# The normalised x of tokens 1024 to 2047 of a hybrid attention layer: turned by transposing DMAs instead of by TensorE

## The chip, the cores and the metric

One core of a Trainium2 chip. The metric is the device time of one execution in microseconds (us). TensorE (PE) multiplies and can transpose 128x128 blocks, VectorE (DVE), ScalarE (ACT) and GpSimd (POOL) work element by element, SyncE (SP) issues most DMAs. Every engine has its own queue and runs it in order.

## The reference

A decoder layer over 2048 tokens of width 1024, batch 1. Two attention mixers share one normalised, modulated input and one input projection:

```
xn = rms_norm(x, g_pre)                    # per token
h  = xn * (1 + scale(c)) + shift(c)        # per channel, the same for all tokens
q,k,v,f,z (mixer A), q,k,v,z (mixer B) = split(h @ w_in)
A: forgetting attention, 8 heads, causal, all 2048 keys
B: sliding window of 128 with sinks, 8 query heads, 2 key heads, rotary positions
out = x + gate(c) * rms_norm(concat(A * silu(z_A), B * silu(z_B)) @ w_out)
```

The change touches only how `h` comes to stand with channels on partitions, as the projections need it.

## The kernel before, in words

The tokens are cut into four chunks of 512 (`ci` 0 to 3), each into four tiles of 128 tokens x 1024 channels: `xt[0]` to `xt[15]`, loaded by `load_x` (L410). For each chunk `squares` (L417, ACT) sums x squared per token, `root` turns the sums into `rst` = 1/rms (a few small steps on DVE, then a chain on POOL, L108 to L122), and `normal` (L429, DVE) multiplies the tile by it.

`turn(ci, k)`, one of eight per chunk, brings channels k*128 to k*128+127 of the 512 tokens onto partitions: four PE transposes (L435) into `px`, ACT applies the channel's scale `Gp` and shift `Shp` into `hf`, float32 (L441; for even k also into the high part of `hT`), and DVE casts the high part for odd k (L445) and subtracts it from `hf` to give the low part (L446). `hT[ci]` holds both float16 parts, [128, 2, 8, 512]. A projection takes three products: high by high, low by high, high by low of the weight.

`hf` comes from a pool `hst` of three buffers with one tag. `px` comes from PSUM.

Then the projections of mixer B follow chunk by chunk: `kb(ci)`, keys, 24 matmuls (L351 with `wh_kb`); `vb(ci)`, values (L795); then one or more `zb` parts, the gate (L351 with `wh_zb`), whose weights are scaled and split shortly ahead (L267 on ACT, L273 on DVE). `kb(ci)` walks over k and at each k needs all 512 tokens of `hT[ci]`. After `kb` come rope steps: ACT copies the sums into `qf`, four DMAs turn halves around into `qs` (L751), DVE combines them with the tables `cosT` and `sinT` into `stb` (L754 to L765), and four DMAs store that to `kst` (L779). `spread(g)` (L460, L461) is eight loads of the tables of chunk g. Weights' maxima go through DRAM with stores of 4 bytes per partition, `mx_d` (L230), and come back as `mxr` (L235).

The order is written by hand. PE's work is a list of units, `punits`; the turns of the next chunk are set between units. Other work hangs on the number of a unit: `at_slice(n, f)` runs f there, and `after(n, f)` puts f some two units times n later, so that an engine's queue isn't given a step long before its input. The instructions then stand in each engine's queue in the order in which they were written. DMAs on SP signal completion on eight semaphores in turn, and a DMA is issued only when the one eight before it has landed.

Late in the kernel, transposing DMAs (L1483) already bring `o_d` from DRAM into `T`.

Of the kernel before, what the change touches and what calls it, by code (L numbers as in the profile page):

```python
# [43 lines left out]
def hybrid_layer(  # L44
# [32 lines left out]

    o_d = [dram.tile([CH, D], F32, name="o_d0")] + [dram.tile([4, 2, P, D], F16, name=f"o_d{t}") for t in range(1, NCH)]
    z_d = dram.tile([KT, P, S], F32, name="z_d")
    mx_d = [dram.tile([P, 1], F32, name=f"mx_d{n}") for n in range(3)]  # L80


# [58 lines left out]
    def early_pool(name, bufs):  # L141
        return early.enter_context(tc.tile_pool(name=name, bufs=bufs, side="right", reuse_waits="tile"))

    xin, hst, vbw = early_pool("xin", 4), early_pool("hst", 3), early_pool("vbw", 1)
    trig = early_pool("trig", 1)
    swx = ExitStack()
    swc = swx.enter_context(tc.tile_pool(name="swc", bufs=1))

# [53 lines left out]
    def after(n, f):  # L202
        late.append([n, f])
# [215 lines left out]
    def root(ci):  # L419
        ss, rst = rstd[ci]  # L420
        rsqrt_mean(rst, ss[:], 4, G if ci else None)

    def normal(ci, us=range(4)):
        for u in us:
            t, r = ci * 4 + u, rstd[ci][1][:, u:u + 1]
            if ci == 0:
                A.activation(xt[t], xt[t], AF.Copy, scale=r)
            else:
                V.tensor_scalar(xt[t], xt[t], r, None, op0=ALU.mult)  # L429
# [20 lines left out]
    def turn_x(ci, k):  # L450
        scaled, split = turn(ci, k)
        after(1, scaled)
        after(2, split)

    def spread(g):

        gr, gc = slice(32 * g, 32 * g + 32), slice(g * CH, (g + 1) * CH)
        for r in range(4):
            rr = slice(32 * r, 32 * r + 32)
            SP.dma_start(cosT[rr, gc], cs_[gr, :])  # L460
            SP.dma_start(sinT[rr, gc], (sp_ if r % 2 else sn_)[gr, :])  # L461
# [4 lines left out]
    with tc.manual_schedule():  # L466
# [207 lines left out]
            kaps[key] = kappa(pws[key], key)  # L674
        V.tensor_scalar(kf[:], kaps["vb"][:], PS_SCALE, None, op0=ALU.mult)
        normal(1, (0, 1))
        spread(0)
        for t in range(8, 12):
            load_x(t)
    start.close()  # L680
# [281 lines left out]
    def add(key, us):  # L962
        if key in ("va01", "va23"):
            for j in key[2:]:
                add(f"va{j}", [])
        elif key not in pkeys and key not in ("kb", "vb"):
            at = len(punits) - {"za3": 4}.get(key, 20 if key[:2] == "za" else 0)
            for n, (lead, f) in enumerate(((42, lambda: w_load(key, pieces(key))), (31, lambda: w_max(key)),
                                           (21, lambda: w_back(key)), (12, lambda: w_scale(key)),
                                           (9, lambda: w_high(key)), (7, lambda: w_low(key, 0)),  # L970
                                           (5, lambda: w_low(key, 1)), (4, lambda: w_done(key)))):
                if n >= 4 and key[:2] in ("qk", "za"):
                    lead -= 1
                if n < 4 and key == "qb0":
                    lead += (16, 14, 12, 4)[n]
                if key[:2] in ("zb", "va"):
                    lead += {"va0": 26, "va2": 26, "zb3": 18}.get(key, 8)
                if n == 0 and key in ("qk1", "za0"):
                    lead += 8
                if key == "zb1":  # L980
                    lead = at - (6, 38, 46, 67, 71, 73, 75, 77)[n]
                if key == "zb0":
                    if n >= 3:
                        events.setdefault((13, 13, 14, 15, 16)[n - 3], []).append(f)
                else:
                    events.setdefault(max(at - lead, n), []).append(f)
        if key not in pkeys:
            pkeys.append(key)
        punits.extend(us)
# [10 lines left out]
    def at_slice(n, f):  # L1000
        events.setdefault(n, []).append(f)
# [17 lines left out]
    for ci in range(NCH):  # L1019
        n0 = len(punits)  # L1020
        add("kb", kb_units(ci))
        add("vb", vb_units(ci))
        if ci < 3:
            add(*others[ci])
            if ci == 2:
                add(*others[4])
                add(*others[5])

            mine, punits[n0:] = punits[n0:], []
            at_ = ([14, 16, 17, 18, 19, 20, 21, 22], [6, 8, 10, 12, 14, 16, 18, 20], [14, 16, 18, 20, 22, 24, 26, 28])[ci]  # L1030
            for n, u in enumerate(mine):
                punits.append(u)
                if n in at_:
                    punits.append(lambda ci=ci, k=at_.index(n): turn_x(ci + 1, k))
            if ci < 2:

                for u in range(4):
                    at_slice(n0 + (24 if ci else 9) + u, lambda ci=ci, u=u: squares(ci + 2, (u,)))
                    at_slice(len(punits) + (4 if ci else -10) + u, lambda ci=ci, u=u: normal(ci + 2, (u,)))
                at_slice(len(punits) - (3 if ci else 18), lambda ci=ci: root(ci + 2))  # L1040
            at_slice((12, 22, 30)[ci], lambda ci=ci: spread(ci + 1))
    n0 = len(punits)
    at_slice(n0, lambda: open_fox())
# [740 lines left out]
```

## Time and profile before

| | us |
|---|---|
| median of 3 runs | 1157.98 (1157.04 to 1157.98) |
| profiled execution, its time | 1157.8 |
| its span | 1156.1 |
| PE busy, share of the span | 1116.8 (97%) |
| DVE busy | 930.5 (80%) |
| ACT busy | 661.4 (57%) |
| POOL busy | 207.5 (18%) |
| mean granted clock of PE | 0.996 of full |

Busy times are of instructions only; the time in which an engine waits is not in them. The part of the program that the change touches runs from about 20 to 130 us.

### The profile page before, as it was taken

What the parts mean: (1) busy time and instruction counts of PE and PEld (TensorE: products, weight loads), DVE (VectorE), ACT (ScalarE), POOL (GpSimd) and SP (SyncE); (2) the same over time, 40 slices, a digit from 0 to 9 for tenths busy, and PEclk for the clock granted to TensorE, in tenths of its full rate; (3) what the DMA queues carried; (4) which work ended last, traced back from release to release, by engine and by line L of the source; (5) the groups of instructions that cost most, each with busy time, mean ns of one, the idle gap of its engine ahead of it and who ended that gap; (6) DMA issues with size and microseconds to landing.
All of it is one profiled execution on the core that took longest, in us unless ns stands there. A gap on an engine that the chain in (4) does not pass through costs nothing. (4 is left out here: it accounts for less than half of the span.)

```text
span 1156.1 us, 25291 instructions
## 1 busy us (share of the span) xinstructions
PE 1116.8 (97%) x9869; PEld 656.3 (57%) x9869; DVE 930.5 (80%) x2137; ACT 661.4 (57%) x1150; POOL 207.5 (18%) x332
## 2 busy tenths in 40 slices
PE   5899999999999999999999999999999999999997
PEld 2475544577765866555555555555555555544444
DVE  7877468987888568788988899888888887878885
ACT  2876344654555421666757666666776778534332
POOL 1122134554556530010010110001000000000000
PEclk9899999999999999999999999999999999999999
DMA  9943355433243232442344342123311337686743
GB/s 333 336 116 72 87 78 96 97 63 90 52 92 88 58 87 58 73 108 29 80 64 87 84 67 70 38 49 76 45 43 34 91 101 206 140 225 197 199 135 109
DMA packets 123476, 120.10 MB, mean 104 GB/s; under 512 B 64948, under 2 KB 100828, under 8 KB 123356
## 3 DMA queue, kind: packets, MB, share of 16 engines
q1 hardware_dynamic: 112088, 85.69, 27.6%
q0 software_dynamic: 10832, 32.50, 13.5%
q8 instruction: 77, 1.26, 0.6%
q14 instruction: 43, 0.35, 0.1%
q10 hardware_dynamic: 436, 0.28, 0.1%
HBM read 64.75 MB, written 25.18 MB: 78 GB/s over the span
## 5 line engine op out<-in xcount | busy, mean ns | idle before, releaser
L1356 ACT ACTIVATE p<-sta,lift,scl_qk 128x1024 f32<-128x1024 f32 (+2 forms) x160 | 172.0, 1075 | 131.6 <-PE sta L1350 82.6
L351 PE MATMUL bk<-hT,wh_qk 128*128 128x512 f16 x768 | 194.7, 378 | 0.0
L1363 DVE TENSOR_TENSOR pha<-p,pha 128x1024 f16<-128x1024 f32 (+2 forms) x160 | 169.1, 1057 | 0.2 <-ACT pha L1360 0.2
L1303 DVE TENSOR_REDUCE a_m<-bk 128x1 f32<-128x512 f32 x192 | 130.4, 686 | 45.8 <-PE bk L1300 44.8
L1576 PE MATMUL bk<-wohl,oz 128*128 128x512 f16 x744 | 165.3, 379 | 1.1 <-DVE oz L1525 0.7
L1360 ACT ACTIVATE pha<-p 128x1024 f16<-128x1024 f32 (+2 forms) x160 | 148.1, 926 | 5.9 <-PE poa L1376 1.2
L1576 PEld LDWEIGHTS <-oz 128*128 128x128 f16 x744 | 71.9, 99 | 82.8 <-DVE oz L1525 1.8
L1376 PE MATMUL poa<-vt,pha 128*128 128x65 f16 x1088 | 116.1, 192 | 1.4 <-DVE pha L1363 1.2
L1373 PE MATMUL poa<-vt,pha 128*128 128x65 f16 x1088 | 116.6, 193 | 0.8 <-DVE ona L1382 0.7
L1375 PE MATMUL poa<-vt,pha 128*128 128x64 f16 x1088 | 116.6, 194 | 0.0
L351 PEld LDWEIGHTS <-wh_qk 128*128 128x128 f16 x768 | 72.1, 97 | 74.4 <-issue 2.1
L1349 PE MATMUL sta<-T 128*128 128x512 f16 (+1 forms) x320 | 110.9, 346 | 2.8 <-ACT p L1356 2.7
L1300 PE MATMUL bk<-T 66*128 66x512 f16 (+2 forms) x320 | 109.7, 348 | 2.4 <-DVE a_m L1303 1.9
L1373 PEld LDWEIGHTS <-pha 128*128 128x128 f16 x1088 | 101.5, 96 | 15.5 <-DVE ona L1382 1.9
L1350 PE MATMUL sta<-T 69*128 69x512 f16 (+1 forms) x320 | 109.8, 348 | 0.0
L1375 PEld LDWEIGHTS <-pha 128*128 128x128 f16 x1088 | 100.9, 97 | 11.4
L1376 PEld LDWEIGHTS <-pha 128*128 128x128 f16 x1088 | 100.8, 99 | 1.8 <-DVE pha L1363 1.7
L351 PE MATMUL bk<-hT,wh_za 128*128 128x512 f16 x384 | 99.7, 378 | 0.0
L369 PE MATMUL bk<-wh_va,hT 128*128 128x256 f16 x768 | 91.9, 273 | 0.0
L351 PE MATMUL bk<-hT,wh_zb 128*128 128x512 f16 x384 | 91.6, 379 | 0.2 <-DVE qc L754 0.2
L351 PE MATMUL bk<-hT,wh_qb 128*128 128x512 f16 x384 | 91.2, 379 | 0.0
L369 PEld LDWEIGHTS <-hT 128*128 128x128 f16 x768 | 73.3, 98 | 12.2 <-issue 2.1
(459 smaller groups left out, 1919.7 us busy)
## 6 DMA issues: line engine op xcount, KB each, us to landing
hT<-in_x_dram SPq DMA_DIRECT2D x20, 512.0 KB
wa<-in_w_ada_dram SPq DMA_DIRECT2D x16, 512.0 KB
z_d<-tz POOLq DMA_DIRECT2D x32, 256.0 KB, 3.0
T<-z_d SPq DMA_DIRECT2D x16, 512.0 KB
T<-stq SPq DMA_DIRECT2D x62, 128.0 KB
out_dram<-hT SPq DMA_DIRECT2D x15, 512.0 KB
xt<-in_x_dram SPq DMA_DIRECT2D x12, 512.0 KB
qs<-qf SPq DMA_DIRECT2D x80, 64.0 KB
```

Of the source, the lines that this page charges most:

```text
L351: PE.matmul(ps, whl[:, a, k, :], hT[ci][:, b, k, :], start=(k == 0 and n == 0), stop=(k == KT - 1 and n == 2))
L369: PE.matmul(ps[:, (u % 2) * 2 * P:(u % 2 + 1) * 2 * P], hT[ci][:, a, k, u * P:(u + 1) * P], wv[p][:, b, k, :], start=(k == 0 and n == 0), ...
L1303: V.tensor_reduce(m3[:, u, pc:pc + 1], mx[:, :w], axis=AX.X, op=ALU.max)
L1349: PE.matmul(self.st[:, o:o + w], T[:, 3, kb_], T[:, 1, qc], start=True, stop=False)
L1350: PE.matmul(self.st[:, o:o + w], T[0:XR, 2, kb_], T[0:XR, 0, qc], start=False, stop=not diag)
L1356: A.activation(self.p32[:, :self.w], self.st[:, :self.w], AF.Exp, scale=scl[f"qk{self.hd}"][:], bias=lift[:])
L1360: A.activation(self.ph[:, 0, :self.w], self.p32[:, :self.w], AF.Copy)
L1363: V.tensor_tensor(self.ph[:, 1, :self.w], self.p32[:, :self.w], self.ph[:, 0, :self.w], op=ALU.subtract)
L1373: PE.matmul(po[:, u, :], ph[:, 0, pq], vt[:, b, hd, 0:65], start=(self.first and n == 0 and u == 0), stop=False)
L1375: PE.matmul(po[:, u, 0:64], ph[:, 0, pq], vt[:, b, hd, 65:VW], start=False, stop=False)
L1376: PE.matmul(po[:, u, :], ph[:, 1, pq], vt[:, b, hd, 0:65], start=False, stop=(self.last and n == len(self.blocks) - 1))
L1576: PE.matmul(py, self.hl[:, i, k, :], w_slot(8 * j + k)[:, cc], start=(k == 0 and m_ == 0), stop=(k == KT - 1 and m_ == 2))
```

## The change

For chunks 2 and 3 (tiles `xt[8]` to `xt[15]`) the turns, and `normal`, are gone. `flat(ci, u)` takes their place, one per tile of 128 tokens, while tokens are still on partitions: DVE multiplies by `rst` and by `rowG`, the scales as one row repeated over partitions; the shifts `rowS` are added (POOL for chunk 2, DVE for chunk 3); ACT copies the result to a float16 tile `hh`, the high part; DVE subtracts it into a second `hh`, the low part; and SP issues two transposing DMAs from the two `hh` into `hT[ci]`. Below, T(ci,u) are these two DMAs, and low(ci,u) and hi(ci,u) the two steps that feed them.

`rowG` and `rowS` come about by a round trip: SP stores `Gp` and `Shp` to DRAM (`g_d`), 128 partitions x 8 pieces of 4 bytes each, ahead of `spread(0)`, and loads them back with a partition broadcast after it. `hh` shares tag and pool, so the three buffers, with `hf`. `squares`, `root` and the four steps of `zb1`'s weights get other slots. Line numbers shift; the function names above hold for both.

```diff
@@ -77,6 +77,7 @@
 
     o_d = [dram.tile([CH, D], F32, name="o_d0")] + [dram.tile([4, 2, P, D], F16, name=f"o_d{t}") for t in range(1, NCH)]
     z_d = dram.tile([KT, P, S], F32, name="z_d")
+    g_d = dram.tile([2, D], F32, name="g_d")
     mx_d = [dram.tile([P, 1], F32, name=f"mx_d{n}") for n in range(3)]
 
 
@@ -142,7 +143,8 @@
         return early.enter_context(tc.tile_pool(name=name, bufs=bufs, side="right", reuse_waits="tile"))
 
     xin, hst, vbw = early_pool("xin", 4), early_pool("hst", 3), early_pool("vbw", 1)
-    trig = early_pool("trig", 1)
+    trig, rowp = early_pool("trig", 1), early_pool("rowp", 1)
+    rowG = rowp.tile([P, D], F32, name="rowG")
     swx = ExitStack()
     swc = swx.enter_context(tc.tile_pool(name="swc", bufs=1))
 
@@ -451,6 +453,21 @@
         scaled, split = turn(ci, k)
         after(1, scaled)
         after(2, split)
+
+    def flat(ci, u):
+
+        t, r = ci * 4 + u, rstd[ci][1][:, u:u + 1]
+        parts = [hst.tile([P, D], F16, tag="hf", name="hh") for _ in range(2)]
+        V.scalar_tensor_tensor(xt[t], xt[t], r, rowG[:], op0=ALU.mult, op1=ALU.mult)
+        (G if ci == 2 else V).tensor_tensor(xt[t], xt[t], rowS, op=ALU.add)
+
+        def low():
+            V.tensor_tensor(parts[1][:], xt[t], parts[0][:], op=ALU.subtract)
+            for b in range(2):
+                SP.dma_start_transpose(hT[ci][:, b, :, u * P:(u + 1) * P], parts[b][:])
+
+        after(2 if ci == 2 else 1, lambda: A.activation(parts[0][:], xt[t], AF.Copy))
+        after(3 if ci == 2 else 2, low)
 
     def spread(g):
 
@@ -674,7 +691,12 @@
             kaps[key] = kappa(pws[key], key)
         V.tensor_scalar(kf[:], kaps["vb"][:], PS_SCALE, None, op0=ALU.mult)
         normal(1, (0, 1))
+        rowS = vbw.tile([P, KT, VB], F32, tag="wraw", name="rowS")[:].rearrange("p k n -> p (k n)")[:, 0:D]
+        for n, (col_, row_) in enumerate(((Gp, rowG[:]), (Shp, rowS))):
+            SP.dma_start(g_d[n].rearrange("(k p) -> p k", p=P), col_[:])
         spread(0)
+        for n, row_ in enumerate((rowG[:], rowS)):
+            SP.dma_start(row_, g_d[n].partition_broadcast(P))
         for t in range(8, 12):
             load_x(t)
     start.close()
@@ -978,7 +1000,7 @@
                 if n == 0 and key in ("qk1", "za0"):
                     lead += 8
                 if key == "zb1":
-                    lead = at - (6, 38, 46, 67, 71, 73, 75, 77)[n]
+                    lead = at - (6, 38, 46, 57, 61, 63, 65, 67)[n]
                 if key == "zb0":
                     if n >= 3:
                         events.setdefault((13, 13, 14, 15, 16)[n - 3], []).append(f)
@@ -1027,17 +1049,16 @@
                 add(*others[5])
 
             mine, punits[n0:] = punits[n0:], []
-            at_ = ([14, 16, 17, 18, 19, 20, 21, 22], [6, 8, 10, 12, 14, 16, 18, 20], [14, 16, 18, 20, 22, 24, 26, 28])[ci]
+            at_ = [14, 16, 17, 18, 19, 20, 21, 22] if ci == 0 else []
             for n, u in enumerate(mine):
                 punits.append(u)
                 if n in at_:
                     punits.append(lambda ci=ci, k=at_.index(n): turn_x(ci + 1, k))
             if ci < 2:
-
                 for u in range(4):
-                    at_slice(n0 + (24 if ci else 9) + u, lambda ci=ci, u=u: squares(ci + 2, (u,)))
-                    at_slice(len(punits) + (4 if ci else -10) + u, lambda ci=ci, u=u: normal(ci + 2, (u,)))
-                at_slice(len(punits) - (3 if ci else 18), lambda ci=ci: root(ci + 2))
+                    at_slice((9, 44)[ci] + u * (1 + ci), lambda ci=ci, u=u: squares(ci + 2, (u,)))
+                    at_slice((24, 58)[ci] + (5 + ci) * u, lambda ci=ci, u=u: flat(ci + 2, u))
+                at_slice((14, 54)[ci], lambda ci=ci: root(ci + 2))
             at_slice((12, 22, 30)[ci], lambda ci=ci: spread(ci + 1))
     n0 = len(punits)
     at_slice(n0, lambda: open_fox())
```

SP, where the x loads of chunk 2 and 3 stand, before: `xt_523` to `xt_529` are tiles 8 to 11, `xt_564` to `xt_570` tiles 12 to 15, and the table loads ahead of them are `spread(0)`.

```order
L460 DMA cosT<-cs__234 32x512
L461 DMA sinT<-sp__232 32x512
L410 DMA xt_523<-in_x_dram 128x1024
L410 DMA xt_525<-in_x_dram 128x1024
L410 DMA xt_527<-in_x_dram 128x1024
L410 DMA xt_529<-in_x_dram 128x1024
L410 DMA xt_564<-in_x_dram 128x1024
L410 DMA xt_566<-in_x_dram 128x1024
L410 DMA xt_568<-in_x_dram 128x1024
L410 DMA xt_570<-in_x_dram 128x1024
L751 DMA qs<-qf 32x512 x4
L460 DMA cosT<-cs__234 32x512
```

The same place now; tiles 8 to 11 are `xt_533` to `xt_539`, and 12 and 13 are loaded earlier, ahead of the stores:

```order
L477 DMA cosT<-cs__239 32x512
L478 DMA sinT<-sp__237 32x512
L699 DMA rowG<-g_d 128x1024
L699 DMA rowS<-g_d 128x1024
L412 DMA xt_533<-in_x_dram 128x1024
L412 DMA xt_535<-in_x_dram 128x1024
L412 DMA xt_537<-in_x_dram 128x1024
L412 DMA xt_539<-in_x_dram 128x1024
L412 DMA xt_578<-in_x_dram 128x1024
L412 DMA xt_580<-in_x_dram 128x1024
L773 DMA qs<-qf 32x512 x4
```

The two row loads stand between `spread(0)` and the x loads, and two stores (`g_d<-Gp`, `g_d<-Shp`) ahead of `spread(0)`.

SP from the end of `spread(3)` on, before:

```order
L461 DMA sinT<-sp__232 32x512
L751 DMA qs<-qf 32x512 x4
L779 DMA kst_556<-stb 64x2x512 x2
L779 DMA kst_557<-stb 64x2x512 x2
L751 DMA qs<-qf 32x512 x4
L779 DMA kst_556<-stb 64x2x512 x2
L779 DMA kst_557<-stb 64x2x512 x2
```

And now; `hT_114` is `hT[2]`, `hT_115` is `hT[3]`:

```order
L478 DMA sinT<-sp__237 32x512
L467 DMA_TRANSPOSE hT_114<-hh 128x8x128 x4
L773 DMA qs<-qf 32x512 x4
L467 DMA_TRANSPOSE hT_114<-hh 128x8x128 x2
L801 DMA kst_566<-stb 64x2x512 x2
L801 DMA kst_567<-stb 64x2x512 x2
L467 DMA_TRANSPOSE hT_115<-hh 128x8x128 x2
L773 DMA qs<-qf 32x512 x4
L467 DMA_TRANSPOSE hT_115<-hh 128x8x128 x4
L801 DMA kst_566<-stb 64x2x512 x2
L801 DMA kst_567<-stb 64x2x512 x2
L467 DMA_TRANSPOSE hT_115<-hh 128x8x128 x2
```

The rows before are rope moves and key stores alone; now T(2,1), T(2,2), T(2,3) and chunk 3's four pairs stand among them, and the key store of kb(2), the last two `kst` rows here, stands ahead of T(3,3). T(2,0) stands ahead of `spread(3)`.

ACT around the last turns of chunk 1, before, with the semaphores that a row waits for; `hT_108` is `hT[1]` and `hT_109` `hT[2]`; the rows with L441 are of k = 5, 6, 6 and 7 of chunk 1 and, the last, of chunk 2:

```order
L441 ACTIVATE hf<-px,Shp,Gp 128x512 [waits DVE_49,PE_49]
L441 ACTIVATE hT_108<-px,Shp,Gp 128x512 [waits PE_49]
L441 ACTIVATE hf<-px,Shp,Gp 128x512 [waits DVE_49,Activation_49]
L441 ACTIVATE hf<-px,Shp,Gp 128x512 [waits DVE_49,PE_49]
L396 ACT_TABLE_LOAD
L396 ACTIVATE tz<-bk_136,cz_zb_761 128x512 [waits PE_49]
L441 ACTIVATE hT_109<-px,Shp,Gp 128x512 [waits PE_49]
```

And now, where `hT_113` is `hT[1]`; `xt_533`, `xt_535` and `xt_537` are tiles 8, 9 and 10, and a name that begins with DMAHW is the landing of a DMA from SP:

```order
L469 ACTIVATE hh<-xt_533 128x1024 [waits Pool_49]
L443 ACTIVATE hf<-px,Shp,Gp 128x512 [waits DVE_49,PE_49,Activation_49]
L443 ACTIVATE hT_113<-px,Shp,Gp 128x512 [waits PE_49]
L443 ACTIVATE hf<-px,Shp,Gp 128x512 [waits DVE_49,Activation_49]
L469 ACTIVATE hh<-xt_535 128x1024 [waits DVE_49,Pool_49]
L443 ACTIVATE hf<-px,Shp,Gp 128x512 [waits DMAHW5_49,PE_49]
L398 ACT_TABLE_LOAD
L398 ACTIVATE tz<-bk_141,cz_zb_771 128x512 [waits PE_49]
L469 ACTIVATE hh<-xt_537 128x1024 [waits Activation_49,Pool_49]
```

The last `hf` of chunk 1 now waits for a DMA, the first of T(2,0), whose source `hh` holds the buffer that it takes.

## The prediction

> **What bounds the kernel now.** The page's busy shares come first, then TensorE's timeline from 44 to 150 us, where the edited work stands.
>
> ```profile
> PE 1116.8 (97%) x9869; PEld 656.3 (57%) x9869; DVE 930.5 (80%) x2137; ACT 661.4 (57%) x1150; POOL 207.5 (18%) x332
> ...
> 61.82 0.81 PE L351 MATMUL bk<-hT,wh_zb 128*128 128x512 f16 x3
> ...
> 76.97 0.87 PE L795 MATMUL bk<-wh_vb,hT 128*128 128x136 f16 x12
> ...
> 85.05 0.60 PE L435 MATMUL px<-ident,xt 128*128 128x128 f32 x4
> 85.49 1.46 PE L351 MATMUL bk<-hT,wh_zb 128*128 128x512 f16 x6
> ...
> 90.90 4.70 PE L351 MATMUL bk<-hT,wh_kb 128*128 128x512 f16 x21
> 97.02 0.38 PE L351 MATMUL bk<-hT,wh_kb 128*128 128x512 f16 x1 [1.43 <-DVE hT L445]
> 97.75 0.59 PE L351 MATMUL bk<-hT,wh_kb 128*128 128x512 f16 x2 [0.35 <-DVE hT L446]
> 98.18 5.13 PE L795 MATMUL bk<-wh_vb,hT 128*128 128x136 f16 x84
> ...
> 123.63 5.34 PE L351 MATMUL bk<-hT,wh_kb 128*128 128x512 f16 x24
> ```
>
> TensorE is busy 97% of the span, so a microsecond that it loses or gains near 100 us reaches the end, unless it runs into a wait there. kb(2) stood 1.43 + 0.35 us for the last pieces of hT[2]; kb(3) at 123.63 stood for nothing. One turn takes 85.49 − 85.05 = 0.44 us of TensorE.
>
> Second, SyncE's queue, where the new transfers will stand.
>
> ```profile
> 46.72 4.49 SPq L410 DMA_DIRECT2D xt<-in_x_dram  x8
> ...
> 59.56 0.51 SPq L460 DMA_DIRECT2D cosT<-cs__234  x1
> 61.43 0.51 SPq L461 DMA_DIRECT2D sinT<-sp__232  x1
> ...
> 69.99 0.58 SPq L461 DMA_DIRECT2D sinT<-sp__232  x1
> 70.69 2.66 SPq L779 DMA_DIRECT2D kst<-stb  x4
> 73.39 0.60 SPq L460 DMA_DIRECT2D cosT<-cs__234  x1
> 74.04 0.59 SPq L461 DMA_DIRECT2D sinT<-sn__233  x1
> ...
> 78.53 2.44 SPq L751 DMA_DIRECT2D qs<-qf  x4
> ...
> 1023.50 2.87 SPq L1483 DMA_TRANSPOSE T<-o_d  x2
> ...
> L1483 SPq DMA_TRANSPOSE T<-o_d x24: 1244/1480/3466, 981.3 to 1098.6; - x24
> ```
>
> SyncE's DMAs signal on eight semaphores in turn, so each stands until the eighth before it has landed. That dates two landings: the third and fourth table loads, at 59.56 and 61.43, are the eighth behind the seventh and eighth x loads, which thus land 12.8 and 14.7 us after the first is issued.
>
> **What is removed.** 16 turns: 16 × 0.44 = 7.0 us of TensorE, and with them kb(2)'s 1.8 us of waits. If nothing else came late, 1157.8 − 8.8 = 1149.0. (The profiled execution, 1157.8 us, is 1.7 over its span and 0.2 under the median 1157.98; I predict on 1157.8.) What hangs behind the turns on ACT and DVE goes too; it was beside TensorE and is worth only the 1.8 counted. kb(2), and later kb(3), need every part of hT, so the last transposition of a chunk sets the start.
>
> **What is added, in the order in which it bites.**
>
> ```profile
> 44.54 0.23 DVE L663 TENSOR_SCALAR Shp<-shf,ipH 128x8 f32<-128x8 f32 x1
> ...
> 78.78 0.54 POOL L230 DMA_DIRECT2D mx_d<-w_mx  x1 [0.50 <-DVE w_mx L227]
> 86.78 0.54 POOL L235 DMA_DIRECT2D mxr<-mx_d  x1 [7.47 <-DMA mx_d<-w_mx]
> ...
> o_d<-oh POOLq DMA_DIRECT2D x24, 128.0 KB, 3.5
> ...
> 60.04 0.20 ACT L417 ACTIVATION_READ_ACCUMULATOR junk<-xt 128x1 f32 x1
> 60.13 1.14 ACT L267 ACTIVATE wh_zb<-wr_zb,w_sw 128x1024 f16<-128x1024 f32 x1
> ```
>
> *1. The rows of scale and shift.* SyncE now holds spread(0) and six x loads behind two stores of Gp and Shp, ready at 44.8. A store of 4-byte pieces exists already: 86.78 − 78.78 = 8.0 us until its reader goes. Plain stores land in 3.5 us; I take 8.0, the row of the same form, and keep 3.5 below. So the stores land at 52.8 and 53.4, the seventh and eighth table loads of spread(0) wait for them, and the row loads go at 54.0, with the x loads behind. Two row loads and six x loads of the same size then land like the eight before: the last two 12.8 and 14.7 us on, at 66.7 and 68.6, xt11, the sixth, near 65.2. ACT squares xt11 by 66.4 (before 60.24), and wh_zb's first piece stands behind it: 66.4 + 1.14 = 67.5. zb starts 5.7 us late against 61.82.
>
> *2. SyncE until the first transposition.* spread(1)'s fourth load waits for xt15, 68.6; twelve more follow at 0.63 (73.39, 74.04), until 76.8; kst, 2.7, until 79.5; then T(2,0), two transposing DMAs.
>
> ```profile
> 1024.00:1025.00 1.00, 1.00 (x8) 0.62 (x7) 0.47 (x3) 0.81 (x3) 0.00 (x0) 1.00 0.99 356
> ...
> 1025.50:1029.00 3.50, 3.50 (x17) 1.57 (x16) 2.73 (x11) 0.46 (x1) 0.00 (x0) 1.00 1.02 166
> ```
>
> No transposition out of SBUF is in the trace. The nearest row is the pair from DRAM at 1023.50: SyncE gives 2.87 us to the two, and the queues are still on them at 1029.0, 5.5 us after the issue; I put the first at 4.1 (one 1.4 earlier). While plain loads run, the queues at a share of 0.99 move 356 GB/s; while the pair runs, at 1.02, they move 166. [...]
>
> *3. The buffer ring.* hf of a turn and the two hh of flat(2,u) share three buffers. The last hf of hT[1] can be written only when T(2,0)'s first DMA has landed, 83.6, and low(2,1), ahead of its split on DVE, needs the second, 85.0.
>
> ```profile
> L446 DVE TENSOR_TENSOR hT<-hf,hT 128x512 f16<-128x512 f32 x32 | 22.0, 692 | 5.5 <-ACT hf L441 5.0
> ...
> L445 DVE CAST hT<-hf 128x512 f16<-128x512 f32 x16 | 6.8, 426 | 0.3 <-ACT hf L441 0.2
> ...
> L523 DVE SCALAR_TENSOR_TENSOR acc<-wa,sil,acc 128x1024 f32<-128x1024 f32 x4 | 5.1, 1283 | 1.2 <-DMA wa<-in_w_ada_dram 1.2
> ...
> L1363 DVE TENSOR_TENSOR pha<-p,pha 128x1024 f16<-128x1024 f32 x96 | 116.8, 1217 | 0.2 <-ACT pha L1360 0.2
> ...
> L1360 ACT ACTIVATE pha<-p 128x1024 f16<-128x1024 f32 x96 | 101.2, 1054 | 2.1
> ...
> L934 POOL TENSOR_SCALAR_AFFINE_SELECT ptb<-fold 128x512 f16<-128x512 f16 x64 | 48.3, 754 | 0.0
> ```
>
> So 85.0 + 1.2 (low) + 0.4 + 0.7 = 87.3, and kb(1)'s last matmuls end at 88.0 against 76.97: 11.0 us late. That delay contains step 1's.
>
> *4. T(2,1) to T(2,3) one by one.* spread(3), eight loads, holds SyncE from 82.4 to 87.4; T(2,1) 87.4, first half landed 91.5, both 92.9. flat(2,2): DVE comes free at 88.0 (87.3 and 0.7 for a tz), scale 1.3, GpSimd's add 1.5 to 2 (twice the 128x512 row; an estimate), ACT's copy 1.05: 92.4, then T(2,2). [...] low(2,3) waits for its first half, 96.5; T(2,3) at 97.7, landed 103.2. kb(2), without a wait, could start at 88.0 + (90.90 − 76.97) − 7 × 0.44 = 98.8. It starts at 103.2, ends near 108.4, and is 10.2 late against 98.18.
>
> *5. Chunk 3.* Here DVE bounds.
>
> ```profile
> 96.34 0.22 POOL L108 TENSOR_SCALAR rs_v<-rs_v 128x4 f32<-128x4 f32 x1 [9.02 <-DVE rs_h L106]
> ...
> 100.44 0.20 POOL L122 TENSOR_TENSOR rst<-rs_t,rs_y 128x4 f32<-128x4 f32 x1
> ...
> 103.65:112.25 8.60, 8.25 (x55) 5.28 (x56) 8.12 (x20) 4.74 (x9) 0.55 (x1) 1.00 0.31 78
> ```
>
> root(3) stands behind the rope of kb(1), whose qs goes out behind T(2,2), 95.3 to 97.7, landing near 99.5; with two products DVE reaches root near 101.5, GpSimd's chain takes 4.3 (96.34 to 100.64): 105.8. DVE then has, until kst of kb(2), which stands ahead of T(3,3) on SyncE: the 8.12 of that window less about 1.8 of conversions that go = 6.3; four scalings, four adds, three subtractions, 4 × 1.28 + 7 × 1.22 = 13.7; two waits for ACT's copy, 2.1. That is 127.9; kst 2.7; the pair 5.5: hT[3] is whole at 136.1. kb(3) could have started at 108.4 + (123.63 − 98.18) − 8 × 0.44 = 130.3. It starts 136.1 − 123.63 = 12.5 late. The stall that is left is 5.8 us.
>
> *6. The clock.*
>
> ```profile
> 45.69 0.38 PE L351 MATMUL bk<-hT,wh_kb 128*128 128x512 f16 x1 [1.90 <-ACT hT L441]
> ...
> 48.00:50.00 2.00, 2.00 (x6) 0.63 (x5) 1.78 (x4) 2.00 (x4) 1.67 (x5) 0.50 0.88 307
> ```
>
> After 1.90 us of idle TensorE ran at half clock, through 48 to 50; I read some 3.4 us of it, costing 1.7. I add 1.7 once, for kb(3)'s stall; the same after kb(2)'s lies inside that stall.
>
> **Sum.** 1157.8 + 12.5 + 1.7 = 1172.0. Bounds: stores at 3.5 instead of 8.0, −4.5; pairs that land like plain loads, −4 over the three on the path; no clock loss, −1.7: 1162. Above: a second clock loss, 1.7, and DVE standing for ACT twice more and GpSimd's adds at double my price, about 6: 1180.
>
> **Rivals.**
> *A, SyncE held longer (0.13).* A transposition out of SBUF takes SyncE twice the 1.44 us of the DRAM one. T(2,0), T(2,2) and T(3,3) each add 2.9 in issue, T(2,1) 0.7: 1172 + 9.4 = 1181 to 1182. For it: the 24 rows of the DRAM form range to 3.5 us. Against: their median is 1.48. [...]
> *B, the rows come late (0.08).* The 1024 pieces per store land in 24 us, three times the 128 pieces' 8.0: +16, 1188.
> *C, faster: the transfers stay under cover (0.14).* If T(3,3) has landed when TensorE arrives, only zb's late start is paid. It decides at about 122: T(3,3) must be there 14 us before step 5 has it, so SyncE must reach T(2,0) near 70 and DVE must do flat(3,u) between its other work. Then the 8.8 are kept less the part of 5.7 that squares cannot recover, some 4: 1153. For it: SyncE and the queues (share 0.31 in the window above) have idle time. Against: every step of the serial chain.
> *D, a tie (0.05):* half of the chain's delay hides, 1158.
>
> **How the numbers follow.** The likeliest is the main chain, 0.60, 1172, its own range 1162 to 1180. The range 1158 to 1188 leaves out C and half of B, about 0.18. A measurement tells 0.2%, 2.3 us, from no change. Faster 0.14, same 0.05, slower 0.81.
>
> **What would show it.** In the changed kernel's trace: the row loads issued near 54; T(2,0) near 79 and not 70; a wait inside kb(1)'s last matmuls on hT; kb(2) standing for a DMA, near 103; kb(3) standing some 6 us, near 136, with the clock at half behind it; from there on every row 14 us later than before. I am wrong if kb(3) starts before 124, or if kb(2) and kb(3) stand for DVE or ACT and not for a transposition.

## The result, and the profile after

The changed kernel takes 1191.33 us (median of four runs, 1188.07 to 1192.13) against 1157.98 (1157.04 to 1158.40): a ratio of 1.0284, with an interval of 1.0263 to 1.0305. It is slower by 33 us. The profiled execution took 1188.07 us, its span is 1186.3, and the mean granted clock fell from 0.996 to 0.977. The later runs stood beside the kernel before on other chips, where that took 1155.6 to 1158.8; kernels are therefore compared by their ratios.

The page of the changed kernel, busy times:

```profile
PE 1122.2 (95%) x9805; PEld 655.1 (55%) x9805; DVE 941.1 (79%) x2125; ACT 653.9 (55%) x1134; POOL 218.9 (18%) x336
```

TensorE has 16 turns less to do (64 transposes, 7.0 us), and yet it is busy for 5.4 us longer: the same matmuls took 12.4 us more, at a lower clock. Outside its busy time lie 1186.3 − 1122.2 = 64.1 us of idleness, before 1156.1 − 1116.8 = 39.3. So −7.0 + 12.4 + 24.8 = +30.2, which is the difference of the spans.

TensorE's timeline of the changed kernel, with what ended each wait in brackets:

```profile
68.38 0.48 PE L437 MATMUL px<-ident,hT 128*128 128x128 f32 x1 [6.35 <-DVE hT L431]
...
86.62 2.16 PE L353 MATMUL bk<-hT,wh_kb 128*128 128x512 f16 x4 [3.76 <-DVE hT L447]
...
91.69 1.74 PE L353 MATMUL bk<-hT,wh_kb 128*128 128x512 f16 x3 [1.74 <-DVE hT L447]
...
109.76 0.38 PE L353 MATMUL bk<-hT,wh_kb 128*128 128x512 f16 x1 [4.01 <-DVE fl L831]
...
112.93 7.04 PE L353 MATMUL bk<-hT,wh_kb 128*128 128x512 f16 x23 [2.78 <-DMA hT<-hh]
...
146.52 0.61 PE L353 MATMUL bk<-hT,wh_kb 128*128 128x512 f16 x1 [5.34 <-DMA hT<-hh]
...
151.39 6.59 PE L353 MATMUL bk<-hT,wh_kb 128*128 128x512 f16 x23 [4.25 <-DMA hT<-hh]
```

Four places stall: the last turn ahead of zb (6.35), kb(1) (3.76 + 1.74), kb(2) (4.01 + 2.78) and kb(3) (5.34 + 4.25), 28.2 us together; the kernel before stood 1.8 us at kb(2). The queue of SyncE in the changed kernel:

```profile
45.28 0.53 SPq L696 DMA_DIRECT2D g_d<-Shp  x1
...
53.79 0.51 SPq L477 DMA_DIRECT2D cosT<-cs__239  x1
...
55.57 0.58 SPq L699 DMA_DIRECT2D rowG<-g_d  x1
...
82.28 3.08 SPq L467 DMA_TRANSPOSE hT<-hh  x2
...
103.53 6.90 SPq L467 DMA_TRANSPOSE hT<-hh  x2
...
138.07 3.20 SPq L801 DMA_DIRECT2D kst<-stb  x4
141.37 4.42 SPq L467 DMA_TRANSPOSE hT<-hh  x2
```

Then the windows view, one row for a stretch (width, busy time of PE, PEld, DVE, ACT and POOL, granted clock, DMA share, GB/s), first of the kernel before:

```profile
60.00:80.00 20.00, 19.19 (x154) 13.13 (x152) 18.10 (x37) 15.17 (x24) 5.87 (x15) 1.00 0.50 121
80.00:100.00 20.00, 18.22 (x161) 12.31 (x159) 10.91 (x29) 13.30 (x24) 3.47 (x12) 1.00 0.21 44
100.00:130.00 30.00, 29.64 (x217) 18.16 (x215) 19.10 (x39) 13.62 (x23) 5.75 (x11) 1.00 0.41 98
130.00:165.00 35.00, 35.00 (x240) 18.62 (x238) 20.64 (x57) 13.12 (x29) 4.01 (x7) 1.00 0.44 75
```

and of the changed one:

```profile
60.00:80.00 20.00, 13.65 (x100) 9.91 (x98) 11.84 (x29) 12.30 (x22) 7.40 (x14) 0.83 0.69 233
80.00:100.00 20.00, 14.06 (x113) 9.07 (x111) 17.42 (x16) 8.42 (x10) 8.83 (x6) 0.74 0.59 128
100.00:130.00 30.00, 23.20 (x175) 13.27 (x173) 19.03 (x37) 11.28 (x21) 7.39 (x18) 0.89 0.88 129
130.00:165.00 35.00, 25.40 (x179) 14.01 (x178) 14.87 (x43) 7.46 (x14) 3.07 (x5) 0.85 0.50 94
```

One of the four places lies in each of these stretches, and in each the clock is below 1. With windows of 2.5 us, the busy time times the missing part of the clock is 2.0, 3.6, 2.0 and 1.8 us in the four, against 0.0 in all four before: 9.4 of the 12.4. Some 2 us more (5.3 against 3.2) lie between 20 and 60 us, ahead of the first stall, behind two stalls of 3.97 and 1.9 us that the kernel before has too. Another 1.6 lie from 987 to 991 us, far behind the edit, after waits of 0.99 and 0.71 us. (This way of counting is rough: the parts come to 13.1, not 12.4.)

### The profile page after: what moved, and what is told of

Read it like the earlier page. It is cut to its first block, busy times and chain, and to the rows that moved or that the text cites. A ratio compares the mean times of both kernels' runs of the same rounds, so it can differ in the third digit from the quotient of the medians.

```text
span 1186.3 us, 25169 instructions
## 1 busy us (share of the span) xinstructions
PE 1122.2 (95%) x9805; PEld 655.1 (55%) x9805; DVE 941.1 (79%) x2125; ACT 653.9 (55%) x1134; POOL 218.9 (18%) x336
```

## The experiments

### What each part costs

Two kernels do a part of the change alone. The first is the kernel before with only the stores of `Gp` and `Shp` and the two row loads; all turns stay.

```diff
...
+        for n, (col_, row_) in enumerate(((Gp, rowG[:]), (Shp, rowS))):
+            SP.dma_start(g_d[n].rearrange("(k p) -> p k", p=P), col_[:])
         spread(0)
+        for n, row_ in enumerate((rowG[:], rowS)):
+            SP.dma_start(row_, g_d[n].partition_broadcast(P))
```

> Edit: the kernel before, with only the two stores of Gp and Shp and the two row loads added at the places of the change; nothing reads the rows, and all turns stay. Theory (the rows alone cost what zb's late start shows, and no later wait gives it back): zb starts near 70, and all later work is 8 us late: near 1164. Rival (the 8 us are cover for what would have waited anyway, kb(2)'s 1.8 us for example): 1156 to 1160.

The second uses `flat` for chunk 2 and turns for chunk 3; its first lines (behind them, chunk 3's `squares`, `root` and `normal` go back to their places):

```diff
-            at_ = [14, 16, 17, 18, 19, 20, 21, 22] if ci == 0 else []
+            at_ = ([14, 16, 17, 18, 19, 20, 21, 22], [], [14, 16, 18, 20, 22, 24, 26, 28])[ci]
...
```

> Edit: chunk 2 as in the change, chunk 3 turned by TensorE as before. It divides the loss: rows 8 us, chunk 2 some 12 less the 5 that its turns and waits cost, chunk 3 the rest. By the starts of vb(2) in the changed kernel (119.8 against 98.2, and 3.5 us of chunk 3's turns come back behind it): near 1180, so chunk 3 costs about 10. If chunk 2's delay only hid chunk 3's, above 1186.

Rows alone: 1.0070 (1.0055 to 1.0085), some 8 us. Rows and chunk 2: 1.0220 (1.0203 to 1.0237), some 25. With chunk 3, the whole change, 33. So the rows are worth 8, chunk 2 another 17, chunk 3 another 7 to 8 (by the intervals, each step is good to some 3 us). The page and TensorE's timeline of the kernel with the rows alone:

```profile
PE 1122.0 (96%) x9869; PEld 659.9 (57%) x9869; DVE 928.9 (80%) x2137; ACT 661.6 (57%) x1150; POOL 207.8 (18%) x332
```

```profile
69.10 0.47 PE L437 MATMUL px<-ident,hT 128*128 128x128 f32 x1 [6.29 <-DVE hT L431]
```

The stall ahead of zb is there whole, without a single transposing DMA, and the same 9869 matmuls are busy for 5.2 us longer than before. That is most of the 7.1 us by which this execution's span grew (1163.2 against 1156.1); idle time grew by 1.9 only, so other waits gave back some 4 of the 6.29.

### Transposing or plain, ring, GpSimd, tables

Four edits of the changed kernel, one at a time. A plain DMA of the same bytes in place of the transposing one (the tokens are then not turned):

```diff
-                SP.dma_start_transpose(hT[ci][:, b, :, u * P:(u + 1) * P], parts[b][:])
+                SP.dma_start(hT[ci][:, b, :, u * P:(u + 1) * P], parts[b][:].rearrange("p (k n) -> p k n", n=P))
```

> Edit: the sixteen transposing DMAs become plain DMAs of the same bytes between the same tiles, so the turning is left out of chunks 2 and 3; order and waits are the same. Theory (order and waits, not the speed of a transposition, make the time): within 4 us of 1191, with kb(2) and kb(3) still waiting. Rival (transposing is slow and holds up its neighbours in the queues: the rope copies qs behind T(2,2) landed 4 us late, and T(3,3) took 9 us): 10 us or more come back, 1181 or below.

A ring of four, and the low part written into the tile's own memory instead of a second `hh`:

```diff
-    xin, hst, vbw = early_pool("xin", 4), early_pool("hst", 3), early_pool("vbw", 1)
+    xin, hst, vbw = early_pool("xin", 4), early_pool("hst", 4), early_pool("vbw", 1)
...
-        parts = [hst.tile([P, D], F16, tag="hf", name="hh") for _ in range(2)]
+        parts = [hst.tile([P, D], F16, tag="hf", name="hh")[:], xt[t].bitcast(F16)[:, 0:D]]
```

> Edit: the pool shared by hf and hh gets a fourth buffer, and the low part is written over its own x tile, so that flat(ci,u) takes one buffer of the ring and not two. Theory (serial chain through the buffer ring, the main case of the prediction): the last hf of chunk 1 and the lows of chunk 2 no longer stand for landings; kb(1)'s second stall (1.74 us) and T(2,3)'s wait (about 4 us) go, some 5 us in all: near 1186. Rival (VectorE and GpSimd slow each other in chunk 2): the waits were cover for that, and the time stays within 2 us of 1191.

The shifts of chunk 2 added by VectorE:

```diff
-        (G if ci == 2 else V).tensor_tensor(xt[t], xt[t], rowS, op=ALU.add)
+        V.tensor_tensor(xt[t], xt[t], rowS, op=ALU.add)
```

> Edit: the shift row of chunk 2 is added by VectorE and not by GpSimd. Theory (VectorE and GpSimd hold each other up): the casts and subtractions that took 2.6 to 3.3 us beside GpSimd's adds come back to 0.4 to 1.3, kb(1)'s first stall (3.76 us) goes, 3 to 5 us in all: near 1187. Rival (VectorE is the bound, and 1.22 us more per tile delay it): 1191 to 1196.

And `spread(2)` and `spread(3)` later:

```diff
-            at_slice((12, 22, 30)[ci], lambda ci=ci: spread(ci + 1))
+            at_slice((12, 47, 86)[ci], lambda ci=ci: spread(ci + 1))
```

> Edit: the table loads of chunks 2 and 3 go out after the transpositions of their neighbours (slots 47 and 86 instead of 22 and 30). Theory (SyncE's row of 24 table loads holds T(2,0) and T(2,1)): T(2,0) goes near 77 instead of 82, T(2,1) right behind its source, kb(1) and kb(2) gain 4 to 6 us; with chunk 3's chain hanging on the same queue, near 1186. Rival (VectorE's steps for chunk 2 are as late as SyncE): under 2 us, 1189 to 1192.

The ratios are 1.0244 (1.0229 to 1.0259) for the plain DMAs, 1.0278 (1.0262 to 1.0293) for the ring, 1.0274 (1.0243 to 1.0305) for VectorE's adds and 1.0302 (1.0285 to 1.0319) for the later tables: each alone leaves 28 us or more of the 33. VectorE's adds do shorten the first wait that the change brought into kb(1), from 3.76 to 2.17 us. VectorE's timeline of the changed kernel, with the add on GpSimd that ran from 83.12 for 3.16 us:

```profile
84.01 2.56 DVE L447 CAST hT<-hf 128x512 f16<-128x512 f32 x1
```

and with the add on VectorE:

```profile
83.60 0.42 DVE L447 CAST hT<-hf 128x512 f16<-128x512 f32 x1
```

The same conversion, last input of kb(1)'s first waiting matmul, takes 2.56 us beside GpSimd's add, ending 0.3 us behind it, and 0.42 without; by what the add holds it up is not shown. vb(1) starts at 90.6 instead of 93.2, but the total hardly moves: kb(2) and kb(3) still wait for DMAs, and the last pair lands later (below).

The ring holds VectorE at one place, ahead of kb(2). low(2,3) writes the buffer that T(2,2)'s first transfer reads. VectorE's timeline of the changed kernel, and of the kernel with four buffers:

```profile
107.94 1.23 DVE L465 TENSOR_TENSOR hh<-xt,hh 128x1024 f16<-128x1024 f32 x1 [7.84 <-ACT junk L419]
```

```profile
100.95 1.23 DVE L465 TENSOR_TENSOR xt<-xt,hh 128x1024 f16<-128x1024 f32 x1 [2.73 <-ACT hh L469]
```

The name in the first bracket is a step that merely ended at the same time: T(2,2)'s first transfer landed at 107.76 by its semaphore. VectorE's copies of vb(1) (`fl`), for which kb(2)'s first matmul waits 4.01 us, stand behind this wait. Four buffers take this wait away (the 2.73 us that are left are for the step's own input), and T(2,3) is issued earlier, yet it lands at 111.6 instead of 112.9, so kb(2) goes on only 1.3 us sooner.

A likely reason for T(2,2)'s late landing stands on GpSimd's queue; its timeline in the changed kernel:

```profile
97.11 0.56 POOL L232 DMA_DIRECT2D mx_d<-w_mx  x1
...
105.80 0.56 POOL L237 DMA_DIRECT2D mxr<-mx_d  x1 [4.08 <-DMA mx_d<-w_mx]
```

T(2,0)'s two transfers landed 3.2 and 3.1 us after their issue (plain ones 2.9 and 3.1); T(2,2)'s took 9.5 and 8.3, beside this store of 128 pieces of 4 bytes, in flight from 97.11 to 105.53. In all 18 kernels here that use `flat`, T(2,2)'s first transfer was issued within 1.4 us of that store and landed 0.2 to 2.9 us after the store did. No run moves the store, so that it is the cause is not shown.

### The way of the rows

The stores and row loads on GpSimd's queue, off SyncE's:

```diff
-            SP.dma_start(g_d[n].rearrange("(k p) -> p k", p=P), col_[:])
+            G.dma_start(g_d[n].rearrange("(k p) -> p k", p=P), col_[:])
...
-            SP.dma_start(row_, g_d[n].partition_broadcast(P))
+            G.dma_start(row_, g_d[n].partition_broadcast(P))
```

> Edit: the two stores of Gp and Shp and the two row loads are issued by GpSimd and not by SyncE; the x loads go out as in the kernel before. Theory (the rows hold up SyncE): zb begins near 62 instead of 70, the first transposition near 74 instead of 82, and the whole 8 us come through: near 1183. Rival (kb(3) is bounded by VectorE and by the last transposition whatever comes ahead): zb comes back to 62, and the time gains under 3 us.

The same with ring and VectorE's adds:

> Edit: the three before together. If the three delays are independent and on the path, they add to 17 us: near 1174. If one chain at the end of chunk 3 (kst of kb(2) ahead of the last transposition on SyncE, and its landing) takes back what comes ahead, it stays above 1180. Below 1158 only if transposing itself was no cost at all.

1.0306 (1.0250 to 1.0363) and 1.0201 (1.0184 to 1.0218). zb is back at 62.4 and 61.7, as before the change, but the wait comes back inside zb; TensorE's timeline of the second:

```profile
76.08 1.11 PE L437 MATMUL px<-ident,hT 128*128 128x128 f32 x4 [7.03 <-ACT hf L443]
```

The other way is to keep the order and make the pieces long: TensorE turns `Gp` and `Shp`, so that a store has 8 pieces of 512 bytes instead of 1024 of 4. First with the transposes at the stores:

```diff
...
+            PE.transpose(bk[0][0:KT, (2 + n) * P:(3 + n) * P], col_[:], ident[:])
+            V.tensor_copy(gT[:, n * P:(n + 1) * P], bk[0][0:KT, (2 + n) * P:(3 + n) * P])
-            SP.dma_start(g_d[n].rearrange("(k p) -> p k", p=P), col_[:])
+            SP.dma_start(g_d[n].rearrange("(k p) -> k p", p=P), gT[:, n * P:(n + 1) * P])
```

> Edit: Gp and Shp are first turned by TensorE into 8 rows of 128 channels, so that the two stores write 512-byte pieces and not 4-byte ones; places on SyncE unchanged. Theory (thousands of 4-byte writes choke the queues: the 2 KB packets behind them took 0.8 us each from 48 to 51 us): the table loads behind them are quick again, x loads go near 50 instead of 56.8, zb starts near 64, all 6 us come through: near 1185. Rival (SyncE's place alone counts, not the size of the pieces): 1189 to 1192.

That gave 1.0303 (1.0280 to 1.0325): where they stood, TensorE waited 9.64 us for the first copy at 57.59, so the price of the pieces can't be read from it. Then with both transposes and one copy right behind the step that makes `Shp`:

> Edit: as the one before with 512-byte stores, but the copy of the turned columns stands right behind Shp on VectorE, so that kb(0) does not wait for it. Theory (4-byte writes choke the queues): x loads near 50 instead of 56.8, zb near 64, 4 to 6 us come through: near 1186. Rival (size of pieces does not matter): 1190 to 1193.

1.0179 (1.0164 to 1.0194): 12 us of the 33 come back. SyncE's queue:

```profile
51.80 0.59 SPq L478 DMA_DIRECT2D sinT<-sp__237  x1
52.43 0.61 SPq L703 DMA_DIRECT2D rowG<-g_d  x1
```

No table load waits for the stores any more, and the row loads go at 52.43 instead of 55.57. TensorE is busy for 1121.7 us, as in the changed kernel (1122.2), so the gain is idle time. Its timeline shows where:

```profile
104.56 0.38 PE L353 MATMUL bk<-hT,wh_kb 128*128 128x512 f16 x1 [1.99 <-DMA hT<-hh]
...
108.67 7.39 PE L353 MATMUL bk<-hT,wh_kb 128*128 128x512 f16 x23 [3.74 <-DMA hT<-hh]
...
140.43 0.49 PE L353 MATMUL bk<-hT,wh_kb 128*128 128x512 f16 x1 [3.15 <-DMA hT<-hh]
...
142.85 7.37 PE L353 MATMUL bk<-hT,wh_kb 128*128 128x512 f16 x23 [1.93 <-DMA hT<-hh]
```

kb(2) goes on 112.93 − 108.67 = 4.3 us earlier, kb(3) 151.39 − 142.85 = 8.5. Up to kb(2) the rows explain it; of the rest, 1.8 us were gained before T(3,3)'s issue (135.24 instead of 141.37) and 2.4 in its landing, which the next part takes up.

### The last pair, and the turning by itself

On this base (long pieces) two kernels: the transposing DMAs replaced by plain ones, and the adds on VectorE. And the changed kernel with `zb2`'s weight load later and issued by ScalarE:

```diff
-            for n, (lead, f) in enumerate(((42, lambda: w_load(key, pieces(key))), (31, lambda: w_max(key)),
+            for n, (lead, f) in enumerate(((42, lambda: w_load(key, pieces(key), A if key == "zb2" else None)), (31, lambda: w_max(key)),
...
+                if key == "zb2" and n == 0:
+                    lead -= -8
```

> Edit: 512-byte stores as in e11_wide2, and plain DMAs of the same bytes in place of the transposing ones; the turning of chunks 2 and 3 is left out. Theory (order and waits count, the turning costs SyncE 0.6 us a DMA and the landing little): 1172 to 1175. Rival (the turning is the cost): 1165 or below.

> Edit: 512-byte stores as in e11_wide2, and the adds of chunk 2 on VectorE. Theory (VectorE and GpSimd hold each other up): the stretched casts go, kb(1)'s stalls of 4.2 and 1.7 us shrink by 2 to 3: 1172 to 1174 against e11's 1176.5. Rival (1.2 us more a tile on VectorE eat it up): 1176 to 1178.

> Edit: the changed kernel, with the load of zb2's weights issued by ScalarE behind kb(3) and vb(3)'s first copies and not by GpSimd beside T(3,3). Theory (that load slows the last pair): T(3,3) lands some 5.5 us after its issue instead of 9 to 10, kb(3)'s second stall shrinks by 3 to 4 us: near 1187, with less scatter. Rival (pieces of 256 bytes are slow beside anything): 1190 or more.

Plain DMAs: 1.0184 (1.0167 to 1.0200) against 1.0179 with transposing ones, so here the turning itself costs no time. SyncE does hold them longer; the DMAs out of `hh` (count, shortest, median and longest in ns), of the changed kernel and of this plain one:

```profile
L467 SPq DMA_TRANSPOSE hT<-hh x16: 1232/1254/2467, 82.3 to 143.3; - x16
```

```profile
L467 SPq DMA_DIRECT2D hT<-hh x16: 593/632/1382, 79.1 to 137.1; - x16
```

The landings of T(2,0) are close too, 3.2 and 3.1 us after the issue against 2.9 and 3.1 for plain ones. Between the changed kernel and its own plain version, though, the ratios differ by 0.0040, and the intervals do not overlap: there the transposing kind cost some 4.6 us, 14% of the 33.

VectorE's adds on the long pieces: 1.0220 (1.0184 to 1.0257), although vb(1) starts at 88.5 instead of 90.3. TensorE's timeline shows where that went:

```profile
151.56 7.07 PE L353 MATMUL bk<-hT,wh_kb 128*128 128x512 f16 x23 [9.71 <-DMA hT<-hh]
```

Its T(3,3) was issued at 135.54, as early as in the kernel beside it (135.24), and landed 8.7 us later. GpSimd's timeline has a weight load of 512 KB between:

```profile
138.14 0.90 POOL L223 DMA_DIRECT2D wr_zb<-in_w_in_dram  x1
```

| kernel | T(3,3) issued | weight load issued behind it | kb(3)'s last wait ends | from the pair's issue |
|---|---|---|---|---|
| VectorE's adds | 139.8 | 2.2 | 155.9 | 16.1 |
| long pieces, VectorE's adds | 135.5 | 2.6 | 151.6 | 16.0 |
| rows on GpSimd's queue | 143.3 | 2.6 | 157.8 | 14.5 |
| later tables | 139.5 | 2.3 | 150.4 | 10.9 |
| ring of four | 140.6 | 2.2 | 150.9 | 10.3 |
| plain DMAs | 141.2 | 2.0 | 151.5 | 10.2 |
| changed kernel | 141.4 | 2.1 | 151.4 | 10.0 |
| long pieces | 135.2 | 4.3 | 142.9 | 7.6 |
| changed, long pieces at their first place | 147.7 | 3.1 | 154.4 | 6.7 |
| changed, weight load later | 141.6 | 17.5 | 148.9 | 7.3 |
| long pieces, plain DMAs | 136.1 | 4.0 | 142.1 | 6.0 |
| rows on GpSimd, ring, VectorE's adds | 136.3 | 5.3 | 142.2 | 5.9 |

With the load 2.0 to 2.6 us behind it, the pair lands after 10 to 16 us; with 3 us or more between them, after 6 to 8, transposing or plain. The one run that moves the load alone takes 2.7 us off (10.0 to 7.3, one profiled execution of each), so the load is a part of the delay. It isn't worth the same in the total: that kernel has 1.0284 (1.0269 to 1.0300), since a later wait of VectorE for the rope of chunk 3, behind which TensorE stood 2.99 us at 183, gave back what kb(3) had gained. What makes 16 of 10 stays open.

### Can the order be mended

All of ring, VectorE's adds, later tables, long pieces (at their first, bad place), and chunk 3's squares, root and `flat` earlier:

```diff
-                    at_slice((9, 44)[ci] + u * (1 + ci), lambda ci=ci, u=u: squares(ci + 2, (u,)))
-                    at_slice((24, 58)[ci] + (5 + ci) * u, lambda ci=ci, u=u: flat(ci + 2, u))
-                at_slice((14, 54)[ci], lambda ci=ci: root(ci + 2))
+                    at_slice((9, 34)[ci] + u * (1 + ci), lambda ci=ci, u=u: squares(ci + 2, (u,)))
+                    at_slice((24, 46)[ci] + (5, 5)[ci] * u, lambda ci=ci, u=u: flat(ci + 2, u))
+                at_slice((14, 42)[ci], lambda ci=ci: root(ci + 2))
```

> Edit: the wider ring with the low part in place, VectorE's adds, the 512-byte stores and the late table loads together, and chunk 3's squares, root and flat in slots 34 to 61 instead of 44 to 76, ahead of the waits of kb(2). If order and waits are the whole cost, all of it can be hidden and the turns' 7 us are gained: 1150 to 1156. If VectorE (3.7 us a tile against 2.6 in the turns) or the landings bound chunk 3 in any order, it stays above 1160.

The same with the long pieces at their second place:

> Edit: as the one before with all remedies together and chunk 3 early, with the copy mended in the same way. That one started kb(0) 12 us late and still reached kb(3) 2 us earlier than the changed kernel; without that delay about 12 us less than its 1183: 1170. It would fall below 1158 if no stall were left in chunk 3; the former had 4.25 us in zb and 3.8 in kb(2), and VectorE was busy throughout, so 1165 to 1172.

1.0238 (1.0223 to 1.0253) and 1.0126 (1.0110 to 1.0143). The second is the best of all, 14.6 us slower than before. TensorE's timeline of it:

```profile
64.89 0.47 PE L437 MATMUL px<-ident,hT 128*128 128x128 f32 x1 [4.08 <-DVE hT L431]
...
81.21 0.38 PE L353 MATMUL bk<-hT,wh_kb 128*128 128x512 f16 x1 [2.39 <-DVE hT L447]
...
93.11 5.34 PE L353 MATMUL bk<-hT,wh_zb 128*128 128x512 f16 x24 [2.02 <-DVE qc L780]
...
102.98 7.99 PE L353 MATMUL bk<-hT,wh_kb 128*128 128x512 f16 x23 [2.50 <-DMA hT<-xt]
...
120.20 18.49 PE L353 MATMUL bk<-hT,wh_zb 128*128 128x512 f16 x72 [3.55 <-DVE qc L780]
```

kb(3) stands for nothing now, but TensorE waits 2.02 and 3.55 us for VectorE's rope, `qc`, where it waited 0.22 at most before. Three more, on this base or on the long pieces: x of chunk 2 ahead of the stores together with the later weight load; the same without the later load; and chunk 3's earlier slots alone.

> Edit: e12_best2 with the x loads of tiles 8 to 11 ahead of the stores and of the row loads, and zb2's weight load moved as in e13. Theory (the rows' place before the x loads costs 4 to 5 us at zb's start): zb starts near 62 instead of 66.5 and the gain comes through: 1164 to 1166 against e12's 1170. Rival (VectorE is the bound behind it, with 3.7 us a tile): 1168 to 1171. Below 1156 under neither.

> Edit: e12_best2 with the x loads of tiles 8 to 11 ahead of the stores and of the row loads; the weight load stays on GpSimd. Theory (e16 lost 8 us behind kb(3) to the moved weight load alone, since its kb(3) started 1.6 us earlier than e12's): ratio near 1.011 against e12's 1.0126. Rival (the x loads first cost it): 1.017.

> Edit: 512-byte stores as in e11_wide2, and chunk 3's squares, root and flat in slots 34 to 61 instead of 44 to 76; buffers, adds and table loads as in the change. Theory (T(3,3) stands behind kb(2)'s store and beside the weight load): kb(3) waits for nothing, its stalls of 3.2 and 1.9 us and the half clock behind them go, about 6 us: ratio to before near 1.013 against e11's 1.018. Rival (VectorE's work moved into chunk 2's stretch delays kb(2) by as much): 1.018 or more.

1.0178 (1.0163 to 1.0193), 1.0151 (1.0128 to 1.0174) and 1.0179 (1.0161 to 1.0197): none gains. With x first (the second of them), zb starts at 62.3, as before the change, and a wait of 3.96 us for ScalarE's `hf` takes its place inside zb. With chunk 3 earlier alone, kb(3) has no wait, and kb(2) waits for 5.98 + 1.94. No version here beats the kernel before. Which of VectorE's own added steps and the transfers holds the last 14.6 us was not settled.

## Why the prediction was right in sign and short in size

The forecast of 1172 was made on the profiled execution of 1157.8, as +14.2. That execution's counterpart came out at +30.3; the median, 1191.33, lies beyond the upper end of the range, 1188. The mechanism was the one named in the main: slower, by serial waits on the way to hT. One sign of being wrong came true by half: kb(2) stood 4.01 us for VectorE before it stood 2.78 for a transposition; VectorE itself stood for a transposition then. The gap of 16 us has two parts, in the prediction's own terms.

**Step 6, the clock, is the step that failed.** It counted one drop, 1.7 us, and held that a second would lie inside a stall. The whole loss was 12.4, 10.7 more. All four places had their drop, and together these cost 9.4; the two at zb and kb(1) step 6 did not consider at all. The other 3 us lie at 20 to 60 and at 987 us, where no stall is new and longer than 1 us, and no run here explains them. The drops were also longer than the 3.4 us that step 6 read off the kernel before: by the clock in windows of 0.5 us, the half clock stood from 65.6 to 72.5, 86.1 to 96.3, 110.0 to 116.8 and 144.1 to 154.4, two or three times 3.4 us. In kb(1) the second stall fell into the half clock that the first had brought:

```profile
87.50:90.00 2.50, 2.29 (x5) 0.55 (x4) 0.69 (x1) 1.68 (x3) 0.00 (x0) 0.50 0.44 100
90.00:92.50 2.50, 0.67 (x2) 0.19 (x2) 2.25 (x3) 2.47 (x4) 0.00 (x0) 0.50 0.60 123
```

Shorter stalls, of 1.90 us (the kernel before, at 45.69) and 1.57 us (the rows alone, at 105.79), were followed by the half clock too, while one of 1.90 us at 201.24 of the kernel before and one of 2.02 us in the best order were not. So in these runs the length of a short stall alone does not say whether it costs a drop.

**The waits came to 28.2 us instead of 21.2** (5.7 at zb, 5.3 at kb(1), 4.4 at kb(2) and 5.8 at kb(3)); 1.6 of these 7.0 were made up elsewhere. The terms most out of size are two landings: T(2,2)'s first transfer, taken at 4.1 us, took 9.5 (step 4), and the pair T(3,3), taken at 5.5, took 10.0 (step 5). An undisturbed pair was priced about right: T(2,0)'s landed 4.9 us after the issue of its first. Step by step:

| first matmul of | before | predicted | measured |
|---|---|---|---|
| zb | 61.8 | 67.5 | 70.0 |
| vb(1) | 77.0 | 88.0 | 93.2 |
| vb(2) | 98.2 | 108.4 | 119.8 |
| kb(3), after its last wait | 123.6 | 136.1 | 151.4 |

- Step 1: the stores landed 9.0 and 9.7 us after their issue, not 8.0; the loads that wait for them went at 53.79 and 54.97, the rows at 55.57 (predicted 54.0). Rival B, 24 us for a store, is out. zb's delay was put down to wh_zb behind xt11 on ScalarE. The trace has another step ahead of it, on ScalarE and VectorE:

```profile
62.90 1.06 ACT L419 ACTIVATE junk<-xt 128x1024 bf16<-128x1024 f32 x1 [7.27 <-DMA xt<-in_x_dram]
```

```profile
67.04 0.49 DVE L829 SCALAR_TENSOR_TENSOR vb<-bk,vb 128x128 f16<-128x128 f32 x2 [6.38 <-ACT vb L825]
```

  The square that waits for x stands ahead of vb(0)'s copies, VectorE waits for these, and `normal` and the turn behind it. So the same late x stopped TensorE 6.35 us, and half clock did the rest.
- Steps 2 and 3: T(2,0) went at 82.28 (predicted 79.5), and kb(1) waited on hT as named. Its first wait, though, was the conversion that GpSimd's add stretched from 0.42 to 2.56, and not the ring. With four buffers kb(1)'s second wait, 1.74 us, is gone, yet the total stayed.
- Step 4: T(2,2) went at 98.28 instead of 92.4 and held low(2,3) until 107.94 instead of 96.5, so kb(2) went on at 112.93 instead of 103.2. GpSimd's add, estimated at 1.5 to 2 us, took 2.80 in the mean; its group in the changed kernel:

```profile
L462 POOL TENSOR_TENSOR xt<-xt,rowS 128x1024 f32<-128x1024 f32 x4 | 11.2, 2804 | 5.2 <-ACT hT L443 2.5 <-PE px L437 1.5 <-ACT hh L469 0.8
```

- Step 5: VectorE was through with kst at 138.07 and T(3,3) stood right behind it, as the order said, but at 141.37, 10.8 later than the 130.6 implied; and the pair landed in 10.0 us, not 5.5, beside the weight load.

Rival A is out: a transposing DMA holds SyncE 1.25 us, not twice 1.44, and plain ones take off 4.6 us of the 33 at most. Rival C is out: rows and chunk 2 alone cost 25 us, and kb(3) without a wait (the best order) still leaves 14.6. Of the bounds, the lower of the stores' (3.5 us) was never near; the upper ones held single terms but not their sum. The 4 us for pairs that land like plain loads was the author's estimate, which no run shows by itself; plain DMAs took some 4.6 us off the changed kernel and nothing off the one with long pieces.

## What to carry to other kernels

TensorE was busy for 97% of the span before, and in the changed kernel the waits of 5.5 to 9.6 us at four places cost more than their length: with each came a stretch at half clock, which cost 1.8 to 3.6 us more and has to be counted with it. Two stores of 1024 pieces of 4 bytes each, with their row loads, cost some 8 us ahead of the queue that feeds the critical path; turning them into long pieces first, at a place where no one waits, gave back 12 of the 33 us. Freeing the busiest engine of 7 us by steps that run one after the other over three others pays only where each has a margin, and a wait that is removed by a new order tends to come up one stage later: look for what is late next before counting it.

## What the runs showed of the hardware

- The half clock stood for 3.4 us (twice in the kernel before) or for two or three times as long, and cost 2.0, 3.6, 2.0 and 1.8 us in the four stretches. Stalls of 1.57 and 1.90 us were followed by it, others of 1.90 and 2.02 were not.
- Two stores of 1024 pieces of 4 bytes landed 9.0 and 9.7 us after their issue. Between 20 and 60 us the queues moved 351 GB/s before and 280 with the rows alone; a part of that is loads that went out later.
- A store of 128 pieces of 4 bytes took 8.4 us, and T(2,2)'s transfers beside it landed after 9.5 and 8.3 us, where T(2,0)'s took 3.2 and 3.1.
- A 128x1024 add on GpSimd took 2.80 us in the mean; a VectorE conversion beside one took 2.56 us, and 0.42 with the add on VectorE.
- A transposing DMA of 128x1024 float16 out of SBUF held SyncE 1.25 us against 0.63 for a plain one; on the long pieces that cost nothing in the total, in the changed kernel some 4.6 us.
